# A Strassen scheme with GpSimd weight sums for both MLPs of a hybrid decoder trunk

## The chip, the cores and the metric

One core of a Trainium2 chip runs the whole kernel in one launch. Its engines work side by side, each on its own in-order queue: TensorE (PE), VectorE (DVE), ScalarE (ACT), GpSimd (POOL) and SyncE (SP), which here only issues transfers between DRAM and the on-chip memory. The metric is the device time of one execution in microseconds (us). Three timed runs of the kernel before took 2699.15, 2699.44 and 2701.14 us; the median is 2699.44 us.

## The reference

The input is 1024 tokens of width 1024, in float32. There are two layers, each a mixer and then an MLP, with a norm before and after each part and a sum onto the stream `h`:

```
hn = rms_norm(h, pre_mix_norm[i])
m = ret_ssd_mixer(hn, ...) if i == 0 else s5_mixer(hn, ...)
h = h + rms_norm(m, post_mix_norm[i])
hn = rms_norm(h, pre_mlp_norm[i])
f = jnp.square(jax.nn.relu(hn @ w_up[i])) @ w_down[i]      # w_up 1024 x 4096, w_down 4096 x 1024
h = h + rms_norm(f, post_mlp_norm[i])
```

The mixer of layer 0 has one wide input projection (6672 columns), retention with 4 heads, a state-space part with 16 heads, gates, and an output projection. The mixer of layer 1 (S5) runs a complex diagonal recurrence over the tokens, then `gelu`, then two 1024 x 1024 products, one of which gates the other (the GLU).

## The kernel before, in words

The tokens go through in two blocks of 512. Every large product is made of three fp32r passes over operands that are split into a high and a low part: `split` (L84) copies the tile to fp32r on ACT (L86) and subtracts that from the tile on DVE (L87), and `mm3` (L101) issues the matmuls hi·hi, hi·lo and lo·hi (L103 to L105), each of 128 x 128 by 512 columns. I call these the dense matmuls; there are 10176. Weights come in chunks of half a megabyte: `chunk` (L89) issues one transfer into `raw`, at L93, and splits two tiles of [128, 512], and each tile feeds 12 dense matmuls. `col` makes a product with the weights stationary, `row` one with the activations stationary.

Small work lies beside the large products. `push` registers a generator, and `tick`, which follows each chunk with 5.2 units, advances it a step at a time. The order in which instructions then stand on each engine is the work of the framework's scheduler, which moves an instruction ahead of others whose operands come later. SP holds a single queue in order: an issue that waits for a semaphore holds up every transfer behind it.

The order of stages is: the mixer of layer 0 for block 0 and for block 1 (`mix0`, L544); the MLP of layer 0 for block 0; that of block 1, with the GLU of block 0 put ahead of its last quarter; the MLP of layer 1 for block 0, with the GLU of block 1 inside; the MLP of layer 1 for block 1. `mlp` (L240) works in four quarters of 1024 hidden columns: eight `col` products, relu and square, split into `p2`, then two `row` products that are added into `acc`. A block's hidden values stay on chip. The S5 generator of each block (`s5`, L719) is spread over most of an MLP of 376 us. It goes through eight groups of channels; for each group DVE makes two complex products of six [128, 512] operations (`cmul`, L590 to L597) and eight scans (L762), and then a gelu. The last MLP ends with a column of products tile by tile, so that its norm is taken for one tile of 128 tokens after the other.

GpSimd has only small work: two or three operations on one column for each norm, copies of three columns, and memsets.

## Time and profile before

| | |
|---|---|
| median of three timed runs | 2699.44 us |
| profiled execution: span from the first to the last instruction | 2700.4 us |
| PE busy | 2656.7 us (98%) |
| DVE busy | 1633.3 us (60%) |
| ACT busy | 1128.7 us (42%) |
| POOL busy | 146.1 us (5%) |
| DMA, share of 16 engines | 37.6%, 126 GB/s on average |
[...]

The span is the profiled execution's own time as far as the profile tells it, and it lies within the three timed runs; so nothing has to be added around it. "Busy" counts the time in which at least one instruction of an engine is under way. A busy PE is not PE at its peak, since matmuls overlap. An issue to landing time of a transfer starts when SP issues it and ends when its semaphore rises.

### The profile page before, as it was taken

What the parts mean: (1) busy time and instruction counts of PE and PEld (TensorE: products, weight loads), DVE (VectorE), ACT (ScalarE), POOL (GpSimd) and SP (SyncE); (2) the same over time, 40 slices, a digit from 0 to 9 for tenths busy, and PEclk for the clock granted to TensorE, in tenths of its full rate; (3) what the DMA queues carried; (4) which work ended last, traced back from release to release, by engine and by line L of the source; (5) the groups of instructions that cost most, each with busy time, mean ns of one, the idle gap of its engine ahead of it and who ended that gap; (6) DMA issues with size and microseconds to landing.
All of it is one profiled execution on the core that took longest, in us unless ns stands there. A gap on an engine that the chain in (4) does not pass through costs nothing.

```text
span 2700.4 us, 34267 instructions
## 1 busy us (share of the span) xinstructions
PE 2656.7 (98%) x12424; PEld 2184.6 (81%) x12424; DVE 1633.3 (60%) x3519; ACT 1128.7 (42%) x2047; POOL 146.1 (5%) x374
## 2 busy tenths in 40 slices
PE   7999999999999999999999999999999999999998
PEld 6878878787887778888888888888888888888887
DVE  4657467666647887887464776256377635533334
ACT  4233344333334345543454342365443335444433
POOL 0100111000001010000010000011000001100000
PEclk9999999999999999999999999999999999999999
DMA  5223122522322354444353443255344324432232
GB/s 175 71 86 105 67 86 94 192 82 86 102 77 81 103 192 150 156 167 157 130 204 117 141 156 125 95 179 199 128 152 139 116 93 172 171 126 94 95 101 78
DMA packets 127849, 340.29 MB, mean 126 GB/s; under 512 B 12960, under 2 KB 37792, under 8 KB 127680
## 3 DMA queue, kind: packets, MB, share of 16 engines
q1 hardware_dynamic: 127680, 338.12, 37.6%
q8 instruction: 97, 1.59, 0.2%
q14 instruction: 72, 0.59, 0.1%
HBM read 306.51 MB, written 31.56 MB: 125 GB/s over the span
## 4 chain that ended last, share of the span: by engine, by line
PE 73%; DVE 5%; issue 1%; ACT 1%; DMA 1%; POOL 1%; DVEq 0%; POOLq 0%; ACTq 0%
PE mm L103 22%; PE mm L105 22%; PE mm L104 22%; PE side L748 1%; DVE rope L762 1%; DVE wlo L87 1%; PE side L777 1%; PE side L517 1%; PE side L776 1%; PE side L775 0%; PE side L202 0%; PE side L412 0%; DVE xc L596 0%; POOL sml L134 0%; DVE xc L597 0%
## 5 line engine op out<-in xcount | busy, mean ns | idle before, releaser
L86 ACT CAST whi<-raw 128x512 fp32r<-128x512 f32 x556 | 344.4, 620 | 805.1 <-PE mm L105 454.7
L87 DVE TENSOR_TENSOR wlo<-raw,whi 128x512 fp32r<-128x512 f32 x556 | 381.3, 687 | 420.2 <-ACT whi L86 407.4
L103 PE MATMUL mm<-hT,whi 128*128 128x512 f32 x1472 | 582.6, 396 | 0.7 <-DVE acc L233 0.5
L105 PE MATMUL mm<-hT,wlo 128*128 128x512 f32 x1472 | 580.3, 394 | 0.0
L104 PE MATMUL mm<-hTl,whi 128*128 128x512 f32 x1472 | 577.1, 392 | 0.0
L103 PE MATMUL mm<-whi,p 128*128 128x512 f32 x1248 | 489.2, 392 | 1.7 <-DVE acc L233 1.7
L104 PE MATMUL mm<-wlo,p 128*128 128x512 f32 x1248 | 487.0, 390 | 0.0
L105 PE MATMUL mm<-whi,p 128*128 128x512 f32 x1248 | 486.2, 390 | 0.0
L87 DVE TENSOR_TENSOR wlo<-rs,whi 128x512 fp32r<-128x512 f32 x284 | 195.6, 689 | 281.8 <-ACT whi L86 280.0
L86 ACT CAST whi<-rs 128x512 fp32r<-128x512 f32 x284 | 176.1, 620 | 438.8 <-PE mm L105 306.9
L105 PEld LDWEIGHTS mm<-hT,wlo 128*128 128x128 f32 x1472 | 276.6, 188 | 62.2 <-issue 1.0
L104 PEld LDWEIGHTS mm<-hTl,whi 128*128 128x128 f32 x1472 | 276.7, 188 | 59.5 <-issue 0.5
L103 PEld LDWEIGHTS mm<-hT,whi 128*128 128x128 f32 x1472 | 277.0, 188 | 57.6 <-issue 1.4
L103 PEld LDWEIGHTS mm<-whi,p 128*128 128x128 f32 x1248 | 234.3, 188 | 49.9 <-DVE acc L233 2.2
L105 PEld LDWEIGHTS mm<-whi,p 128*128 128x128 f32 x1248 | 234.3, 188 | 48.9
L104 PEld LDWEIGHTS mm<-wlo,p 128*128 128x128 f32 x1248 | 234.4, 188 | 47.8 <-DVE wlo L87 0.4
L103 PE MATMUL mm<-whi,hT 128*128 128x512 f32 x384 | 155.4, 406 | 0.4 <-ACT whi L86 0.4
L104 PE MATMUL mm<-wlo,hT 128*128 128x512 f32 x384 | 153.3, 399 | 0.5 <-DVE wlo L87 0.5
L105 PE MATMUL mm<-whi,hTl 128*128 128x512 f32 x384 | 152.8, 398 | 0.0
L87 DVE TENSOR_TENSOR p<-tmp,p 128x512 fp32r<-128x512 f32 x128 | 88.1, 688 | 79.7 <-ACT p L86 79.6
L103 PE MATMUL mm<-whi,q 128*128 128x512 f32 x256 | 101.9, 404 | 3.2 <-DVE tmp L434 3.2
L104 PE MATMUL mm<-wlo,q 128*128 128x512 f32 x256 | 101.9, 398 | 1.1 <-DVE wlo L87 1.1
(291 smaller groups left out, 3186.9 us busy)
## 6 DMA issues: line engine op xcount, KB each, us to landing
raw<-in_w_down SPq DMA_DIRECT2D x66, 512.0 KB, 3.3
rs<-in_w_up SPq DMA_DIRECT2D x64, 512.0 KB, 3.3
raw<-in_w_up SPq DMA_DIRECT2D x64, 512.0 KB, 3.2
rs<-in_w_down SPq DMA_DIRECT2D x62, 512.0 KB, 3.3
raw<-in_win_col SPq DMA_DIRECT2D x56, 512.0 KB, 3.3
raw<-in_win_row SPq DMA_DIRECT2D x48, 512.0 KB, 3.2
xt<-h SPq DMA_DIRECT2D x48, 512.0 KB, 4.5
q<-s5m SPq DMA_DIRECT2D x80, 256.0 KB, 2.9
```

The lines of the kernel that those rows point to most:

```text
L86: nc.scalar.copy(hi, src)
L87: nc.vector.tensor_tensor(lo, src, hi.bitcast(F32), op=ALU.subtract)
L103: mm(out, lhs[0], rhs[0], start=first, stop=False)
L104: mm(out, lhs[0], rhs[1], start=False, stop=False)
L105: mm(out, lhs[1], rhs[0], start=False, stop=last)
L517: mm(Y[:, h * 64 : h * 64 + 64], lm[:, h], xd[:, h * 64 : h * 64 + 64], start=True, stop=True)
L748: mm(B[i][:, x], m[i][:, x], u[:, x], start=True, stop=True)
L762: v.tensor_tensor_scan(Z[i][:, x, 1:129], r4, W[i][:, x], Z[i][:, x, 0:1], op0=ALU.mult, op1=ALU.add)
L776: mm(Yv[:, :, x], X[0][:, x], m[3][:, x], start=False, stop=False)
L777: mm(Yv[:, :, x], X[1][:, x], m[4][:, x], start=False, stop=True)
```

## The change

Both MLPs take all 1024 tokens at once. The activations (1024 tokens x 1024) and the weights (1024 x 4096, then 4096 x 1024) are cut into quarters, and the eight products of quarters are replaced by seven over sums of quarters (the Strassen scheme in the form of Winograd). Four of the seven take sums of weights, T1 to T4. They are made by GpSimd (`prep`): 128 steps for each layer, and in each step one transfer of [128, 4, 128] from DRAM, four additions of [128, 128] and one transfer back to DRAM, into `tq`. The tile `prep` has two buffers. The sums of activations are made on DVE: those of the up product by `prenorm_S`, those of the hidden values in `up`, which writes all seven hidden operands to DRAM (`sh`); `up` begins with twenty steps that need block 0 alone (A11·B11 and A12·B21 of ten of its sixteen groups), and finishes the norm of block 1 and its sums (`done`) after them. `down` reads and splits the hidden operands again for each of its seven products; after five of them it hands block 0 to its norm and S5 part, and block 1 after the seventh. The GLUs and the S5 generators no longer lie within an MLP: the S5 part of block 0 lies beside the end of `down` of layer 0, that of block 1 beside the GLU of block 0. Weights now come as tiles of [128, 512] with one transfer each (`wtile`); `raw` has four of them. The buffers of several tags are merged into `k8` and `h2`.

```diff
-            raw=3, whi=3, wlo=3, hT=1, hTl=1, acc=4, xt=2, p2=16, q2=8, nat=8, xc=6, xr=2, tmp=2, lm=2,
-            xx=2, ret=2, kz=2, sml=12, dtt=10, wB=1, rope=2, junk=1, rs=3,
+            raw=4, whi=3, wlo=3, k8=12, xt=2, q2=8, h2=15, lm=2, xx=2, ret=2, kz=2, sml=12, dtt=10, wB=1,
+            rope=2, junk=1, prep=2,
...
+    def wtile(self, src):
+        raw = self.T("raw", [128, 512])
         self.nc.sync.dma_start(raw, src)
+        hi, lo = self.T("whi", [128, 512], F32R), self.T("wlo", [128, 512], F32R)
+        self.split(hi, lo, raw)
+        return hi, lo
...
+    def prenorm_S(self, src, norm, i, b, S):
...
+            self.nc.scalar.copy(a22, P22)
+            v.tensor_tensor(s[0], P21, a22, op=ALU.subtract)
+            v.tensor_tensor(s[2], A11, P21, op=ALU.subtract)
+            v.tensor_tensor(s[1], A11, s[0], op=ALU.subtract)
+            v.tensor_tensor(A12, A12, s[1], op=ALU.subtract)
+            for n, x in (("s3", s[2]), ("s1", s[0]), ("s2", s[1]), ("A22", a22), ("s4", A12)):
...
+    def prep(self, l):
+        nc, g = self.nc, self.nc.gpsimd
+        for u in range(2):
+            for q in range(16):
+                for c in range(4):
+                    s = slice(c * 128, c * 128 + 128)
+                    t = self.T("prep", [128, 4, 128])
+                    nc.sync.dma_start(t, self.a["mlp"][l, u, q, :, :, s].rearrange("b p f -> p b f"))
+                    for d, x in ((0, 1), (1, 3), (3, 0), (2, 3)):
+                        g.tensor_tensor(t[:, d], t[:, d], t[:, x], op=ALU.add)
+                    nc.sync.dma_start(self.tq[l][u, q, :, :, s].rearrange("b p f -> p b f"), t)
+                    yield
...
+    def up(self, l, S, sh, done):
+        ahead = 10
+        def prod(P, g, a, b, first, last):
+            hi, lo = self.wtile(self.weights(l, 0, g, b))
+            for k in range(4):
+                s = slice(k * 128, k * 128 + 128)
+                self.mm3(P, (hi[:, s], lo[:, s]), S[a][k], first and k == 0, last and k == 3)
+            self.tick(2.6)
...
+        for g in range(0, ahead, 2):
+            ahead_of((g, g + 1))
+        done()
+        for g in range(16):
...
+            prod(c, g, "s3", "T3", True, False)
...
+            prod(d, g, "s1", "T1", True, False)
+            v.tensor_tensor(p7, d, p7, op=ALU.subtract)
+            prod(e, g, "s2", "T2", True, True)
+            v.tensor_tensor(V, V, e, op=ALU.subtract)
...
+            for n, x in (("s1", s1), ("s3", A21), ("s2", s2), ("s4", s4)):
+                nc.sync.dma_start(sh[n][g], x)
+
+    def down(self, l, sh, post):
+        def prod(Ps, a, b, first, last):
+            for g in range(0, 16, 2):
+                x = self.K8(F32R)
+                for i in range(2):
+                    raw = self.T("raw", [128, 512])
+                    nc.sync.dma_start(raw, sh[a][g + i])
+                    self.split(x[:, 2 * i], x[:, 2 * i + 1], raw)
+                    w = self.wtile(self.weights(l, 1, g + i, b))
+                    for t in range(4):
+                        s = slice(t * 128, t * 128 + 128)
+                        self.mm3(Ps[t], (x[:, 2 * i, s], x[:, 2 * i + 1, s]), w, first and g + i == 0, last and g + i == 15)
+                    self.tick(2.6)
...
+        self.push(self.prep(0), 128, 600)
...
+        self.up(0, S[0], sh[0], lambda: (self.finish(pre1), self.finish(p[0, 1])))
+        params = self.push(self.s5_params(), 25, 200)
+        self.push(self.prep(1), 128, 560)
...
+        self.down(0, sh[0], post0)
+        for b in range(2):
+            self.finish(s5[b])
+            if b == 0:
+                s5[1] = self.push(s5_run(1), 30, 80)
+            acc = self.glu(y[b])
```

On SP, in the mixer of layer 0 where the input projection's weights come in, the queue of before holds almost nothing but the chunks (names ending in `_row` and `_out` are weights; `lm`, `rope` are small inputs):

```order
L93 DMA raw_492_2250<-in_w_out 128x1024 [waits DMAHW5_49,DMAHW2_49,DVE_49]
L497 DMA lm_738_3288<-cst0_214 128x8x128 [waits DVE_49,PE_49]
L548 DMA rope_942_4247<-in_cos 128x512 [waits DVE_49]
L549 DMA rope_943_4248<-in_sin 128x512 [waits DVE_49]
L93 DMA raw_497_2284<-in_w_out 128x1024 [waits DMAHW3_49,DMAHW1_49,DVE_49]
L93 DMA raw_506_2326<-in_win_row 128x1024 [waits DMAHW4_49,DVE_49]
L93 DMA raw_524_2389<-in_win_row 128x1024 [waits DMAHW5_49,DVE_49]
L93 DMA raw_547_2477<-in_win_row 128x1024 [waits DMAHW1_49,DVE_49]
```

In the changed kernel the same stretch of SP's queue reads like this (`prep` from `in_mlp` is the load of a step's four quarters, `tq0` from `prep` the store of its sums):

```order
L310 DMA prep_518_2476<-in_mlp 128x4x128 [waits DMAHW3_49]
L310 DMA prep_533_2533<-in_mlp 128x4x128 [waits DMAHW5_49]
L101 DMA raw_339_1522<-in_win_row 128x512 [waits DVE_49]
L313 DMA tq0_75<-prep_518_2476 128x4x128 [waits DMAHW6_49,DMAHW1_49,Pool_49]
L101 DMA raw_343_1559<-in_win_row 128x512 [waits DVE_49]
L313 DMA tq0_75<-prep_533_2533 128x4x128 [waits DMAHW7_49,Pool_49]
L310 DMA prep_540_2576<-in_mlp 128x4x128 [waits DMAHW4_49,DMAHW1_49]
L101 DMA raw_346_1565<-in_win_row 128x512 [waits DVE_49]
L310 DMA prep_551_2627<-in_mlp 128x4x128 [waits DMAHW3_49]
L313 DMA tq0_75<-prep_540_2576 128x4x128 [waits DMAHW4_49,Pool_49]
L101 DMA raw_350_1602<-in_win_row 128x512 [waits DMAHW0_49,DVE_49]
L313 DMA tq0_75<-prep_551_2627 128x4x128 [waits DMAHW6_49,Pool_49]
```

Between the weight tiles now stand loads that wait for the landing of an earlier store, and stores that wait for GpSimd (`Pool`). This pattern goes through the whole mixer of layer 0: all 256 steps, those of layer 1 (`tq1`) too, stand ahead of the first weights of `up`, one step to each tile of [128, 512].

On PE, in the S5 part of block 0, the kernel before has 72 or 96 dense matmuls (`mm`) from the transposes of one group of channels (`side` from `nat`, L742) to those of the next. A piece of that:

```order
L105 MATMUL mm_14404<-hT_11908,wlo_14412 128x512
L742 MATMUL side_14453<-c_66,nat_12870 128x128 x4
L103 MATMUL mm_14477<-hT_11908,whi_14480 128x512
L104 MATMUL mm_14477<-hTl_11909,whi_14480 128x512
L105 MATMUL mm_14477<-hT_11908,wlo_14481 128x512
L103 MATMUL mm_14477<-hT_11908,whi_14480 128x512
L104 MATMUL mm_14477<-hTl_11909,whi_14480 128x512
L748 MATMUL side_14460<-xc_14458,q_3007_14443 128x128 x4
L748 MATMUL side_14461<-xc_14458,q_3008_14444 128x128 x4
L105 MATMUL mm_14477<-hT_11908,wlo_14481 128x512
```

In the changed kernel, at the end of `down` of layer 0, the last groups of block 0 follow each other with no dense matmul between them (L920 is the transpose that was L742, L926 was L748, L953 to L955 make the group's output):

```order
L953 MATMUL side_17314<-q_3568_17253,h_3572_17266 128x4x32
L920 MATMUL side_17346<-c_66,k_3298_15994 128x128 x4
L926 MATMUL side_17353<-h_3592_17351,q_3586_17336 128x128 x2
L954 MATMUL side_17314<-q_3569_17254,h_3581_17306 128x4x32
L926 MATMUL side_17353<-h_3592_17351,q_3586_17336 128x128 x2
L926 MATMUL side_17354<-h_3592_17351,q_3587_17337 128x128
L955 MATMUL side_17314<-q_3570_17255,h_3582_17307 128x4x32
```

From the first to the last transposes of a block's S5 part (seven groups) before had 600 dense matmuls for each block; the changed kernel has 264 for block 0 and 202 for block 1. The dense matmuls of the whole program are 9408, where there were 10176.

## Rows read from the trace of the kernel before

**Rows 1.** The page: busy time, share of the span, instructions of each engine.
```profile
PE 2656.7 (98%) x12424; PEld 2184.6 (81%) x12424; DVE 1633.3 (60%) x3519; ACT 1128.7 (42%) x2047; POOL 146.1 (5%) x374
```
**Rows 2.** The page: the chain that ended last, shares of the span by line.
```profile
PE mm L103 22%; PE mm L105 22%; PE mm L104 22%; PE side L748 1%; DVE rope L762 1%; DVE wlo L87 1%; PE side L777 1%; PE side L517 1%; PE side L776 1%; PE side L775 0%; PE side L202 0%; PE side L412 0%; DVE xc L596 0%; POOL sml L134 0%; DVE xc L597 0%
```
**Rows 3.** Six stages: length, busy time (instructions) by engine, PE clock, DMA share, GB/s.
```profile
29.00:505.00 476.00, 469.76 (x2197) 379.34 (x2196) 299.35 (x588) 182.25 (x354) 34.30 (x104) 1.00 0.28 93
505.00:986.00 481.00, 473.34 (x2212) 381.96 (x2211) 331.09 (x748) 188.13 (x368) 39.80 (x107) 1.00 0.32 105
986.00:1362.00 376.00, 375.47 (x1761) 312.74 (x1760) 268.34 (x911) 184.38 (x332) 14.12 (x33) 1.00 0.47 157
1362.00:1852.00 490.00, 487.44 (x2341) 406.17 (x2340) 289.88 (x537) 207.35 (x361) 22.09 (x54) 1.00 0.44 147
1852.00:2341.00 489.00, 487.16 (x2338) 405.42 (x2338) 286.53 (x499) 206.91 (x361) 20.43 (x40) 1.00 0.43 142
2341.00:2691.00 350.00, 350.00 (x1536) 287.99 (x1534) 140.36 (x203) 146.47 (x252) 8.08 (x17) 1.00 0.31 107
```
**Rows 4.** Waits of SP's queue: total us, times, longest.
```profile
SPq L93 <- DVE wlo L87: 1630.7, 353, 13.6
```
**Rows 5.** DMA issues: count, KB each, median us from issue to landing.
```profile
xt<-h SPq DMA_DIRECT2D x48, 512.0 KB, 4.5
...
h<-xt SPq DMA_DIRECT2D x24, 512.0 KB, 3.5
...
s5m<-lm SPq DMA_DIRECT2D x16, 256.0 KB, 2.5
...
xx<-in_s5bc SPq DMA_DIRECT2D x8, 256.0 KB, 2.9
```
**Rows 6.** GpSimd's groups by form: count, busy us, mean ns, idle before.
```profile
L160 POOL TENSOR_TENSOR sml<-sml,c 128x1 f32<-128x1 f32 x32 | 6.1, 191 | 243.7 <-DVE sml L423 243.7
...
L688 POOL MEMSET xc<- 128x512 f32 x8 | 4.2, 528 | 161.6 <-DVE q L594 80.5 <-DVE xc L592 29.4 <-ACT xc L681 24.2
...
L816 POOL MEMSET c<- 128x128 f32 x1 | 0.2, 204 | 0.3 <-POOLq L945 0.3
```
**Rows 7.** The timeline at the start: start us, length us, engine, line.
```profile
9.08 0.19 POOL L158 TENSOR_SCALAR sml<-sml 128x1 f32<-128x1 f32 x1 [8.05 <-ACT junk L169]
...
9.36 0.56 POOL L134 TENSOR_TENSOR sml<-sml,c 128x1 f32<-128x1 f32 x1
...
11.95 1.28 DVE L197 SCALAR_TENSOR_TENSOR acc<-acc,sml,wB 128x1024 f32<-128x1024 f32 x1 [0.72 <-POOL sml L134]
12.00 1.28 POOL L158 TENSOR_SCALAR sml<-sml 128x1 f32<-128x1 f32 x1
```
**Rows 8.** GpSimd's groups between 29 and 986 us, one of them.
```profile
L158 POOL TENSOR_SCALAR sml<-sml 128x1 f32<-128x1 f32 x28 | 9.0, 320 | 237.5 <-ACT junk L169 203.8 <-DVE acc L233 32.3
```
**Rows 9.** DVE's groups by form, those of the S5 part and the split.
```profile
L87 DVE TENSOR_TENSOR wlo<-raw,whi 128x512 fp32r<-128x512 f32 x556 | 381.3, 687 | 420.2 <-ACT whi L86 407.4 <-PE side L742 12.3
...
L762 DVE TENSOR_TENSOR_SCAN rope<-c,rope,xc 128x128 f32<-128x128 f32 x128 | 50.9, 462 | 0.0
...
L594 DVE TENSOR_TENSOR xc<-xc,xc 128x512 f32<-128x512 f32 x32 | 21.8, 681 | 0.0
...
L221 DVE SCALAR_TENSOR_TENSOR nat<-nat,sml,wB 128x512 f32<-128x512 f32 x16 | 11.4, 742 | 3.3 <-POOL sml L163 3.3
...
L784 DVE SCALAR_TENSOR_TENSOR nat<-nat,side 128x512 f32<-128x512 f32 x16 | 11.0, 686 | 7.3 <-ACT nat L783 7.0
...
L781 DVE TENSOR_SCALAR nat<-nat 128x512 f32<-128x512 f32 x16 | 6.8, 427 | 25.0 <-ACT nat L780 25.0
```
**Rows 10.** The timeline at the end.
```profile
2691.30 0.69 DVE L233 TENSOR_TENSOR acc<-mm,acc 128x512 f32<-128x512 f32 x1
...
2694.04 1.42 DVE L221 SCALAR_TENSOR_TENSOR acc<-acc,sml,wB 128x512 f32<-128x512 f32 x2 [2.05 <-POOL sml L134]
2695.37 1.29 DVE L222 TENSOR_TENSOR xt<-xt,acc 128x512 f32<-128x512 f32 x2
```

More of the change, by code (lines that the diff above doesn't have):

```diff
@@ L202, in prenorm_T @@
                     nc.tensor.transpose(P[:, k * 128 : k * 128 + 128], x[:, c : c + 128], self.ident)
-                s = (slice(None), slice(4 * q, 4 * q + 4), slice(t * 128, t * 128 + 128))
-                self.split(hi[s], lo[s], P.rearrange("p (k n) -> p k n", k=4))
+                Ps.append(P.rearrange("p (k n) -> p k n", k=4))
+            yield t, Ps
+    def prenorm_T(self, src, norm, i, hT, early=False):
+        at = []
+        for q in range(2):
+            p, a = self.pair4()
+            hT += p
+            at.append(a)
+        for t, Ps in self.normed(src, norm, i, early):
+            for q in range(2):
+                for hi, lo in at[q](t):
+                    self.split(hi, lo, Ps[q])
+            yield
@@ new lines, in prenorm_S @@
+    def prenorm_S(self, src, norm, i, b, S):
+        v = self.nc.vector
+        if b == 0:
+            at = {}
+            for n in ("A11", "A12"):
+                S[n], at[n] = self.pair4()
+            S["raw"] = []
+            for t, Ps in self.normed(src, norm, i):
+                raw = [self.T("h2", [128, 4, 128]) for _ in range(2)]
+                S["raw"].append(raw)
+                for q, n in enumerate(("A11", "A12")):
+                    self.nc.scalar.copy(raw[q], Ps[q])
+                    for hi, lo in at[n](t):
+                        self.split(hi, lo, raw[q])
+                yield
+            return
+        at = {}
+        for t, (P21, P22) in self.normed(src, norm, i):
+            if not at:
+                for n in ("s3", "s1", "s2", "s4", "A22"):
+                    S[n], at[n] = self.pair4("q2" if n == "A22" else "k8")
+            A11, A12 = S["raw"][t]
+            s = [self.T("h2", [128, 4, 128]) for _ in range(3)]
+            a22 = self.T("h2", [128, 4, 128])
+            self.nc.scalar.copy(a22, P22)
[4 more added lines that the diff above has]
+            for n, x in (("s3", s[2]), ("s1", s[0]), ("s2", s[1]), ("A22", a22), ("s4", A12)):
+                parts = at[n](t)
+                if len(parts) == 1:
+                    self.split(*parts[0], x)
+                else:
+                    for k, (hi, lo) in enumerate(parts):
+                        self.split(hi, lo, x[:, k])
@@ L389, in ret_side @@
         nc, v, mm = self.nc, self.nc.vector, self.nc.tensor.matmul
-        out += [self.T("nat", [128, 512]) for _ in range(4)]
+        o = self.K8()
+        out += [o[:, c] for c in range(4)]
         for hh in range(2):
@@ L462, in conv @@
         nc, v = self.nc, self.nc.vector
-        xr = self.T("xr", [128, 515])
+        xr = self.T("h2", [128, 515])
         if b == 0:
@@ L486, in ssd_side @@
         nc, v, mm = self.nc, self.nc.vector, self.nc.tensor.matmul
-        out += [self.T("nat", [128, 512]) for _ in range(4)]
+        o = self.K8()
+        out += [o[:, c] for c in range(4)]
         S = self.S[g]
@@ L768, in s5 @@
             yield
-            X = [self.T("xc", [128, 4, 128]) for _ in range(2)]
+            X = [self.T("h2", [128, 4, 128]) for _ in range(2)]
             f = lambda y: y[:, :, 0:128]
@@ L880, in run @@
-        del gl["s5"]
-        self.push(after(n1, 1), 2, 60)
-        acc = self.mlp(1, H[4], s5_end(1), free5)
-        post(acc, seq(h3, 0), "post_mlp_norm", 1, str4(out, 0))
-        self.finish(p[5])
-        last = lambda acc: self.postnorm(acc, seq(h3, 1), "post_mlp_norm", 1, str4(out, 1))
-        self.mlp(1, H[5], none, none, last)
+        H = [[], []]
+        self.tq = [self.dr.tile([2, 16, 4, 128, 512], F32, tag=f"tq{l}", name=f"tq{l}") for l in range(2)]
+        self.p1 = self.dr.tile([16, 128, 512], F32, tag="p1", name="p1")
@@ new lines, in run, with pre_S @@
+        names = ("A11", "A12", "A22", "s1", "s2", "s3", "s4")
+        sh = [{n: self.dr.tile([16, 128, 512], F32, tag=f"sh{l}{n}", name=f"sh{l}{n}") for n in names} for l in range(2)]
+        S = [{}, {}]
+        p = {}
+        def pre_S(l, b, src, span):
+            p[l, b] = self.push(self.prenorm_S(src, "pre_mlp_norm", l, b, S[l]), 4, span)
+        self.finish(self.push(self.prenorm_T(seq(x, 0), "pre_mix_norm", 0, H[0], True), 4, 1))
+        self.mix0_setup()
+        self.push(self.prep(0), 128, 600)
@@ L887, in run @@
+        self.up(1, S[1], sh[1], lambda: (self.finish(pre1), self.finish(p[1, 1])))
+        S[1].clear()
+        self.down(1, sh[1], lambda b, acc: post(acc, seq(h3, b), "post_mlp_norm", 1, str4(out, b)))
         self.finish(*list(self.sides))
```

333 lines of the change are left out of this document (190 added, 143 removed).

## The prediction

> **What bounds the kernel now.** I read the busy shares first: PE is busy for 98% of the span, DVE for 60%, ACT for 42%, GpSimd for 5% [rows 1]. The chain of waits says the same: three lines, the dense matmuls L103 to L105, make 66% of it, and no line of another engine has more than 1% [rows 2]. Then the table by stage, because a share of the whole hides stages with different limits. In every stage PE's busy time comes within 7.7 us of the stage's length [rows 3]. The last stage is 1536 dense matmuls and nothing else on PE: 350.0 us, or 0.228 us each, at full clock. So a dense matmul that goes is worth 0.228 us, as long as nothing else sets the pace in its stage. The SP queue tells how much room is left on the side of the weights: its chunks wait for the split that frees a buffer for 1630.7 us in 353 waits [rows 4], so the transfers are early everywhere, and PE is what they wait for in the end.
>
> **The change part by part.** *Removed.* Seven products for eight takes 768 dense matmuls of the MLPs' 6144: 768 x 0.228 = -175 us. That the change does this is certain from the order (9408 for 10176). All rest is what the seven products need beside PE.
>
> *The weight sums, in the mixer of layer 0.* The order puts all 256 steps of `prep` beside the mixer's weights, one to each tile of half a chunk. The mixer's 136 chunks take 957 us, the first two stages in [rows 3], 7.0 us a chunk, in which SP now has to get through two steps as well. A step is a chain: load, four dependent additions, store, and the buffer is loaded again when the store has landed. With two buffers, two steps take one such round. Its parts: a load of 256 KB lands 2.9 us after its issue, a store of the same shape after 2.5 us [rows 5]. The four additions are not in the trace. A two-input operation of one column takes 0.191 us, a memset of 128 columns 0.204 us and one of 512 columns 0.528 us, which is 0.84 ns a column [rows 6]. From below an addition is thus 0.19 + 0.11 = 0.30 us if it streams like a memset; from above, with three streams one behind the other, 0.19 + 0.32 = 0.51 us. I take 0.45, nearer to the upper end since it reads twice. From one dependent GpSimd instruction to the next there are 0.09 us (9.27 to 9.36 us) [rows 7]. GpSimd also waits for DVE: an operation of 0.19 us that starts while DVE runs one with two on-chip inputs takes 1.28 us, exactly as long as that one [rows 7]; in the two mixer stages the mean of this operation is 0.320 us, so 0.13 us of waiting each [rows 8]. Four additions are 4 x 0.54 = 2.2 us without this wait and 2.7 us with it; I take 2.4. With 0.3 us for hand-overs between queues (estimate: three of 0.1 us) the round is 2.9 + 2.4 + 2.5 + 0.3 = 8.1 us. SP is in order: a store that waits for GpSimd holds up the weight tiles behind it, and four `raw` tiles are 14 us of cover, which a steady lag uses up once. So where two steps stand with two tiles, PE gets its tiles every 8.1 us for 7.0. Some 16 chunks have no pair of steps beside them (at the start, at the change of block and at the end, counted in the order), so the 128 pairs of steps share 120 chunks: 128 x 8.1 + 16 x 7.0 = 1149 us for 957, +190 us; GpSimd's queue also holds the norms and the conv's halo copies, which wait for ACT, so I take +200. The bounds: with additions of 0.30 us, no waiting for DVE and hand-overs for nothing the round is 2.9 + 1.6 + 2.5 = 7.0, +50 us (a cost of nothing takes 845 / 128 = 6.6 us); with 0.51 us, the full wait and landings 0.8 us later each it is 10.1 us, +450 us.
>
> [...]
>
> *The S5 parts and the GLU.* DVE needs for one group twelve operations of 0.681 us, eight scans of 0.462 us, and 0.427 + 0.686 + 0.686 us for the gelu [rows 9]: 8.2 + 3.7 + 1.8 = 13.7 us. PE's own part of a group is about 6 us: in the fourth stage PE is busy for 487.4 us, of which 1920 dense matmuls are 437.8, and eight groups share the other 50 [rows 3]. Before, 600 dense matmuls lay between the first and the last transposes of a block, 137 us, and DVE's 96 us for seven groups disappeared beside them. After, there are 264 and 202. Block 0: PE has 60 + 42 = 102 us, DVE 96 us and the splits of 44 tiles at 0.687 us, 30 us: 126 us, 24 us late. Block 1: PE 46 + 42 = 88, DVE 96 + 17 x 0.687 = 108, 20 us late. Nothing covers the ends: block 1 cannot begin before its norm, a store of 3.5 us and a load of 4.5 us [rows 5], about 12 us in all, and after the last group of each block come gelu, transposes and split, about 10 us. Together 24 + 20 + 12 + 20 = 76, +75 us; at least 45 if the ends overlap, 110 if DVE is idle for a tenth of it.
>
> *The start of `up`.* Twenty steps of 12 dense matmuls, 54.7 us, cover the norm of block 1: its tail and way through DRAM, about 15 us, and then four tiles on DVE, each 1.28 us [rows 7], eight operations of 0.69 us and four quarter ones (about 1.1 us), 8 us, 32 us in all, with a quarter of DVE taken by weight splits: 43 us. That is 58 us, and ACT has as much to do: +10 us in each layer, between 0 and +20.
>
> *`up` and `down` themselves.* A group of `up` with five steps is 13.7 us of PE and 15 DVE operations of 0.69 us, 10.3 us; a step of `down` is 2.73 us of PE and two DVE splits, 1.4 us. Both fit, so the work there is hidden by PE. `down` moves 512 KB in 2.73 us, 192 GB/s, and in layer 0 the S5 parameters besides; the third stage ran with 157 GB/s at 0.47 [rows 3]. I take +10 us for late tiles there, up to +40.
>
> *The end.* Before, the last tile of 128 tokens alone was left: from 2691.3 to the end 9 us [rows 10]. Now four tiles finish together: four additions of 0.69 and four times two parts of 0.742 and 0.69 us on DVE [rows 9], 14 us for about 3.5: +10 us.
>
> **The sum**, against the profiled execution's 2700 us, which lies 1 us above the median: 2700 - 175 + 200 + 75 + 20 + 10 + 10 = 2840 us.
>
> **The rivals.** *GpSimd keeps up.* The round is between 6.6 and 7.0 us, or the stores wait so little that four `raw` tiles cover it: the mixer costs 0 to +50 us, the rest stays (75 + 20 + 10 + 10 = 115), and 2700 - 175 + 25 + 115 = 2665 us. For it speaks the room in the queue [rows 4] and that GpSimd is at 5%; against it that even 7.0 us needs both an addition no dearer than a memset and no wait for DVE, of which [rows 7, 8] show some. The point from which it decides is a round of 7.1 us, where the mixer's cost eats up the 60 us that the other terms leave.
>
> *Sharing makes the round much longer.* DVE and GpSimd hold each other up, and the transfers too land later, since `prep` adds 512 KB to a tile's 256 KB. The additions then are 0.75 us each with waiting, 3.0 us, the landings 3.4 and 3.0: 9.7 us, 128 x 9.7 + 112 = 1354, +395 us: 3035 us. For it: the wait in [rows 7]. Against: DVE is busy for only 66% of the two stages, and not always with two on-chip inputs. [...]
>
> **How the numbers follow.** The forecast 0.70, GpSimd keeps up 0.19, much longer 0.11. A measurement tells from no change what is over 0.2%, about 5 us. Forecast's own range: a round of 7.6 to 8.9 us (+125 to +295) with the other terms between 80 and 160 gives 2740 to 2960. Both signs have some chance; the range that should hold 8 in 10 reaches down to the first rival's number and up close to the second's: 2665 to 3010. Faster 0.18 (the first rival but for its worst end, and hardly any of the forecast), same 0.03, slower 0.79.
>
> **What the profile would show.** If I am right: dense matmuls at 0.228 us, 9408 of them; the mixer of layer 0 at about 1150 us with PE busy for some 80% of it, SP's stores into `tq` waiting for GpSimd as its longest waits, GpSimd's additions at about 0.45 us in the mean or more; PE idle by S5's operations of DVE around the GLUs, with some 310 us from the end of `down` to the start of the second `up`. I am wrong if the mixer stays under 1000 us, if additions are 0.3 us, or if weight tiles overtake the stores. Wrong in another way, if PE's granted clock falls below 1.00 where it now pauses: then every stage with pauses would be longer than these terms say.

## The result, and the profile after

The changed kernel takes 3132.57 us (3126.45 to 3137.45, four runs) against 2700.29 us (2699.15 to 2701.58) for the kernel before: 1.159 times as long, 95% interval 1.158 to 1.161. The forecast was 2840 us with a range of 2665 to 3010: the direction is right, the size is not, and the time lies outside the range. The page of the changed kernel, busy time by engine, against [rows 1]:

```profile
PE 2676.1 (85%) x11656; PEld 2131.7 (68%) x11656; DVE 1883.5 (60%) x3919; ACT 1163.8 (37%) x2159; POOL 702.8 (22%) x1410
```

PE is busy for as long as before (2656.7 us) though it has 768 dense matmuls less. The granted clock was 1.00 in every stage before [rows 3]; now it is 0.87 to 0.89 in the stages in which PE is busy for 77 to 82% of the time, 0.97 and 0.98 where it is for 91 and 95%, and 1.00 in the last, where it is for 99.6%. At the lower clock a matmul takes longer: between 44 and 50 us the granted clock is 0.50 and a dense matmul starts 0.43 us after the one before it in the median, between 52 and 66 us it is 1.00 and this takes 0.23 us. The stages of the changed kernel, columns as in [rows 3]: the mixer of layer 0 for both blocks, `up` and `down` of layer 0, S5 and GLU, `up` and `down` of layer 1:

```profile
23.00:711.00 688.00, 531.12 (x2210) 414.82 (x2211) 324.65 (x609) 181.07 (x356) 332.31 (x662) 0.87 0.59 172
711.00:1365.00 654.00, 520.98 (x2213) 410.56 (x2212) 334.36 (x690) 191.37 (x373) 285.28 (x564) 0.89 0.57 167
1365.00:1703.00 338.00, 321.96 (x1379) 257.82 (x1378) 213.32 (x334) 164.48 (x292) 9.83 (x18) 0.98 0.66 217
1703.00:2125.00 422.00, 382.29 (x1771) 305.97 (x1770) 369.32 (x1200) 188.44 (x349) 16.41 (x52) 0.97 0.71 224
2125.00:2460.00 335.00, 273.25 (x1336) 225.22 (x1336) 234.47 (x461) 111.81 (x209) 22.44 (x48) 0.89 0.47 151
2460.00:2799.00 339.00, 323.20 (x1380) 258.20 (x1379) 214.34 (x342) 166.41 (x301) 13.12 (x24) 0.98 0.65 216
2799.00:3115.00 316.00, 314.82 (x1344) 252.34 (x1343) 170.87 (x258) 143.49 (x247) 8.63 (x12) 1.00 0.66 201
```

The mixer of layer 0 takes 1342 us for 957: that is 385 of the 432 us. Its dense matmuls are the same, but PE's granted clock is 0.87 and 0.89 there, a mean over stretches at 1.00 and at 0.50 like those two, and GpSimd is busy for 618 us where it was for 74. The waits of SP's queue in the changed kernel, against [rows 4]:

```profile
SPq L101 <- DVE wlo L93: 457.1, 314, 7.9
SPq L313 <- POOL prep L312: 445.0, 208, 4.0
SPq L310 <- DMA tq<-prep: 170.4, 128, 7.6
SPq L313 <- DMA prep<-in_mlp: 115.3, 100, 6.5
```

Before, weight tiles waited 1630.7 us for a free buffer, so they were early. Now SP also stands at its stores into `tq` (L313) and at the loads of `prep` (L310), and tiles come late: ACT waits 93.4 and 73.8 us for the landing of the input projection's weights (`in_win_row` and `in_win_col`). GpSimd's additions and the landings of `prep` in the changed kernel:

```profile
L312 POOL TENSOR_TENSOR prep<-prep 128x128 f32<-128x128 f32 x1024 | 554.6, 545 | 643.7 <-DMA prep<-in_mlp 584.8
```

```profile
prep<-in_mlp SPq DMA_DIRECT2D x256, 256.0 KB, 3.4
tq<-prep SPq DMA_DIRECT2D x256, 256.0 KB, 2.4
```

The forecast took 2.9 and 2.5 us for the landings and 2.4 us for four additions with their waiting. The loads land half a microsecond later than that; the rest is right, four additions take 2.4 us in the median. What it made of them is not. One passage shows how the pieces lock. GpSimd, then DVE, between 436 and 446 us of the changed kernel, and the next thing that PE waits for (start us, length us, engine, line, and in brackets what the idle time before waited for):

```profile
437.20 2.08 POOL L312 TENSOR_TENSOR prep<-prep 128x128 f32<-128x128 f32 x4 [3.71 <-DMA prep<-in_mlp]
440.21 2.07 POOL L312 TENSOR_TENSOR prep<-prep 128x128 f32<-128x128 f32 x4 [0.92 <-DMA prep<-in_mlp]
442.24 0.19 POOL L165 TENSOR_TENSOR sml<-sml,c 128x1 f32<-128x1 f32 x1
442.51 0.57 POOL L139 TENSOR_TENSOR sml<-sml,c 128x1 f32<-128x1 f32 x1
443.16 0.22 POOL L168 TENSOR_SCALAR sml<-sml 128x1 f32<-128x1 f32 x1
...
436.42 0.18 DVE L598 BATCH_NORM_AGGREGATE sml<-sml 128x2 f32<-128x6 f32 x1
436.82 0.69 DVE L595 SCALAR_TENSOR_TENSOR h<-h,side 128x512 f32<-128x512 f32 x1 [0.21 <-PE side L591]
443.42 0.54 DVE L600 TENSOR_SCALAR k<-side,sml,sml 128x256 f32<-128x256 f32 x1 [5.91 <-POOL sml L168]
443.88 1.28 DVE L93 TENSOR_TENSOR wlo<-raw,whi 128x512 fp32r<-128x512 f32 x2
445.08 0.35 DVE L580 SCALAR_TENSOR_TENSOR ret<-side,c,c 128x128 f32<-128x128 f32 x1
...
445.48 0.70 PE L584 MATMUL side<-k,ret 128*128 128x256 f32 x2 [3.59 <-DVE ret L580]
```

The norm of a retention part (L165, L139, L168) is ready to run at 436.6 us, when DVE's L598 ends. In GpSimd's queue it stands behind eight additions, and the second four wait for their own load: it runs at 442.24. DVE waits 5.91 us for it. Two splits of weight tiles (L93) and a retention operation (L580) stand behind that on DVE, and PE is idle for 3.59 us until L580 is done.

### The profile page after: what moved, and what is told of

It is laid out like the page before. It is cut to its first block, busy times and chain, and to the rows that moved or that the text cites. A ratio compares the mean times of both kernels' runs of the same rounds, so it can differ in the third digit from the quotient of the medians.

```text
span 3134.1 us, 37287 instructions
## 1 busy us (share of the span) xinstructions
PE 2676.1 (85%) x11656; PEld 2131.7 (68%) x11656; DVE 1883.5 (60%) x3919; ACT 1163.8 (37%) x2159; POOL 702.8 (22%) x1410
## 5 line engine op out<-in xcount | busy, mean ns | idle before, releaser
L93 DVE TENSOR_TENSOR wlo<-raw,whi 128x512 fp32r<-128x512 f32 x784 | 553.9, 710 | 555.6 <-ACT whi L92 551.2
L312 POOL TENSOR_TENSOR prep<-prep 128x128 f32<-128x128 f32 x1024 | 554.6, 545 | 643.7 <-DMA prep<-in_mlp 584.8
L108 PE MATMUL mm<-whi,k 128*128 128x512 f32 x1536 | 620.3, 410 | 64.6 <-ACT whi L92 28.5
L109 PE MATMUL mm<-wlo,k 128*128 128x512 f32 x1536 | 626.8, 408 | 34.1 <-DVE wlo L93 33.9
L110 PE MATMUL mm<-whi,k 128*128 128x512 f32 x1536 | 623.7, 407 | 2.7 <-DVE k L93 2.7
L108 PE MATMUL mm<-k,whi 128*128 128x512 f32 x1216 | 493.8, 406 | 55.2 <-ACT whi L92 54.2
L110 PE MATMUL mm<-k,wlo 128*128 128x512 f32 x1216 | 491.1, 405 | 22.1 <-DVE wlo L93 22.0
L109 PE MATMUL mm<-k,whi 128*128 128x512 f32 x1216 | 491.6, 404 | 0.0
L108 PEld LDWEIGHTS mm<-whi,k 128*128 128x128 f32 x1536 | 296.1, 193 | 146.1 <-ACT whi L92 34.0
L109 PEld LDWEIGHTS mm<-wlo,k 128*128 128x128 f32 x1536 | 297.7, 194 | 112.9 <-DVE wlo L93 43.6
L110 PEld LDWEIGHTS mm<-whi,k 128*128 128x128 f32 x1536 | 298.3, 194 | 76.3 <-DVE k L93 5.3
L108 PEld LDWEIGHTS mm<-k,whi 128*128 128x128 f32 x1216 | 234.3, 193 | 117.6 <-ACT whi L92 60.4
L110 PEld LDWEIGHTS mm<-k,wlo 128*128 128x128 f32 x1216 | 233.7, 192 | 83.4 <-DVE wlo L93 28.1
L109 PEld LDWEIGHTS mm<-k,whi 128*128 128x128 f32 x1216 | 233.9, 192 | 54.5 <-issue 0.5
L93 DVE TENSOR_TENSOR k<-raw,k 128x512 fp32r<-128x512 f32 x224 | 153.9, 689 | 102.1 <-ACT k L92 101.0
```

Source lines behind the costliest of these rows:

```text
L93: nc.vector.tensor_tensor(lo, src, hi.bitcast(F32), op=ALU.subtract)
L108: mm(out, lhs[0], rhs[0], start=first, stop=False, skip_group_check=again)
L109: mm(out, lhs[0], rhs[1], start=False, stop=False, skip_group_check=again)
L110: mm(out, lhs[1], rhs[0], start=False, stop=last, skip_group_check=again)
L312: g.tensor_tensor(t[:, d], t[:, d], t[:, x], op=ALU.add)
```

## The experiments

All were run once, next to the kernel before (2699.7 to 2703.6 us). The changed kernel's own four runs differ by 11 us. "The mixer" is always layer 0's, from its first dense matmul to its last. The table gives it in us, to within 1 us, with the whole time; the sections say what was changed.

The scheduler laid out each run's order anew, but for e17 and e18, where an order is imposed. By the traces, e13, e14 and e17 have the changed kernel's order on every engine, and e18 has that of e9. Wherever else the sums or their transfers are kept (e2 to e10, e12, e15, e16), SP's queue at least is in another order than the changed kernel's, so what such a run differs by contains a change of order; what that can be worth is shown by e17 and e18.

| run | whole | mixer | | run | whole | mixer |
|---|---|---|---|---|---|---|
| before | 2700.3 | 957 | | e9 long fills, own order | 2909.1 | 1101 |
| after | 3132.6 | 1342 | | e10 norms off, three buffers | 3076.1 | 1300 |
| e1 no sums | 2772.6 | 979 | | e11 no sums, parameters in up | 2827.0 | 975 |
| e2 transfers issued by GpSimd | 3399.8 | 1594 | | e12 e6, parameters in up | 2975.0 | 1054 |
| e3 transfers alone | 2885.1 | 1085 | | e13 short fills | 2933.4 | 1134 |
| e4 three buffers | 3126.8 | 1328 | | e14 copies | 3004.2 | 1209 |
| e5 additions alone | 3177.7 | 1367 | | e15 e6, more ahead | 2876.3 | 1049 |
| e6 additions on DVE | 2884.2 | 1050 | | e16 e15, S5 under up | 2901.4 | 1050 |
| e7 layer 1's sums later | 3122.3 | 1149 | | e17 long fills, order of after | 3041.2 | 1247 |
| e8 norms off GpSimd | 3116.7 | 1338 | | e18 additions, order of e9 | 3000.9 | 1182 |

### The sums, taken apart

e1, no sums; the products read stored quarters in their place:

```
-        return self.tq[l][u, q, ("T1", "T3", "T4", "T2").index(n)]
+        return self.a["mlp"][l, u, q, ("T1", "T3", "T4", "T2").index(n)]
-        self.push(self.prep(0), 128, 600)
-        self.push(self.prep(1), 128, 560)
```

> The weight sums are left out altogether (prep is not pushed; the four products that want sums read quarters of the weights themselves, with the same sizes), so the output is not the reference's. Theory 1 (the round load, additions, store in SP's in-order queue paces the mixer of layer 0), theory 2 (GpSimd's additions hold up DVE) and theory 3 (the 134 MB of transfers make weight tiles late) all expect the mixer back at about 957 us from 1342, so 3132 - 385 = about 2750 us. What remains above 2700 - 175 = 2525 is then the price of the S5 part, the starts of up, down of layer 0 and the tail. If the loss of the mixer has a cause outside prep (the new buffers, the single tiles of weights), it stays above 1000 us and the total above 2800.

The sums cost 360 us. Without them the kernel is still 72 us slower than before, so the rival "GpSimd keeps up" (2665 us) could not have come out by any speed of the sums.

e3, loads and stores stay, the additions go (`- g.tensor_tensor(t[:, d], t[:, d], t[:, x], op=ALU.add)`):

> The four additions of each step are left out, loads and stores stay in SP's queue; the output is not the reference's. Theory 1: the round is 3.4 + 2.4 + 0.3 = 6.1 us, below the 6.6 us at which it costs nothing; the mixer takes 960 to 1010 us, the total about 2770. Theory 2: the same, about 2750, since no addition is left. Theory 3: the bytes stay, so the mixer stays near 1340 and the total near 3130.

Transfers alone cost 112 us. SP's waits in this run, of its loads for the last store and of its stores for the load, in the first 960 us, show where SP stands (here `prep` is loaded in L310 and stored in L311):

```profile
SPq L311 <- DMA prep<-in_mlp: 286.4, 231, 5.8
SPq L310 <- DMA tq<-prep: 225.4, 225, 5.6
```

Even with nothing to compute SP waits for landings in its own order, with the weight tiles behind.

e5, the additions on two tiles that stay on chip, no transfers (load and store lines taken out):

> Left out: the loads and stores of the weight sums; the same 1024 additions run on GpSimd on two tiles that stay on chip and wait for no transfer, and the products read four of the eight stored quarters in place of the sums. Measure: the two blocks of layer 0's mixer, 957 us before, 1342 us with the change, 979 us without any sums, 1085 us with the transfers alone. Theory A (the round of load, additions and store paces the weight tiles): nothing waits for transfers any more, so 980 to 1000 us. Theory B (the norms and the conv's copies stand in GpSimd's queue behind additions that wait for loads): the additions wait for nothing, a norm is at most 2 to 3 us late, 1000 to 1050 us. Theory C (GpSimd and DVE shut each other out while two on-chip inputs are read): the additions cost what they cost with the change less the transfers' share, 1342 - 106 = 1236 us, and DVE's splits get longer than 0.69 us.

Without a single transfer the additions cost 405 us. That does not settle theory A, though, since most of it is one standstill that the changed kernel does not have. GpSimd and DVE at the start of this run, and then that stretch with the columns of [rows 3]:

```profile
35.79 320.73 POOL L311 TENSOR_TENSOR prep<-prep 128x128 f32<-128x128 f32 x780
...
37.94 318.61 DVE L145 TENSOR_SCALAR dtt<-c 128x16 f32<-128x16 f32 x1
356.46 0.16 DVE L474 TENSOR_SCALAR c<-c 128x16 f32<-128x16 f32 x1
...
36.00:356.00 320.00, 0.86 (x4) 0.30 (x2) 319.52 (x4) 2.34 (x5) 320.00 (x780) 0.50 0.00 1
```

The DVE operation of L145, which takes 0.165 us in the changed kernel, takes 318.61 us here: while GpSimd has these additions one behind the other, it doesn't get in. It ends at 356.55 us, when GpSimd stops at a norm (356.52 us), to wait for DVE. PE works for 0.86 us of these 320. With no transfer to hold them back, 780 of the 1024 additions had gathered there; only some 85 of the 405 us are left for the rest. So the run shows one DVE operation that stayed out over 780 additions in a row, and not how much additions hold DVE up in the changed kernel.

e6, the additions on DVE (`nc.vector` for `g` in L312):

> The additions run on DVE in place of GpSimd; the transfers stay. The order then also puts half of layer 1's sums behind the mixer. A: a round with four additions of about 0.2 us is 3.4 + 0.8 + 2.4 + 0.3 = 6.9 us, no longer than a chunk of PE, so the mixer goes back to that of the transfers alone, about 1085 us or a little more for 100 us more of DVE's time. B: GpSimd's queue is empty again, 1085 to 1110 us. [...] A fourth theory, D (any engine that waits for a load in its own order holds up what stands behind, and on DVE those are the splits themselves): 1200 us or more.

The engine that seemed the fuller one does it for 112 us in all (2884.2 - 2772.6), no more than the transfers alone cost. In its order 98 of the 256 steps lie behind the mixer, so its mixer is not that of e3.

e7, layer 1's sums kept behind the first `up` by a write into their buffers that needs its last tile:

```
+        if l == 0:
+            for _ in range(2):
+                v.tensor_copy(self.T("prep", [128, 4, 128])[:, 0, 0:1], s4[:, 0:1])
```

> The sums of layer 1 are kept behind the first up of layer 0 by a small copy into their buffers; 128 of the 256 steps then lie beside down, S5 and the GLU. A and B: 363 us for 256 steps in the mixer are 182 for 128, so a mixer of about 1160 us; beside down of layer 0 (422 us, where PE waits for DVE and no norm is needed at once) the steps are hidden and cost 0 to 40 us: total 2950 to 3000 us. C: in down DVE is busy for 87%, and 512 additions of 0.55 us that shut it out cost most of that again, +150 to +280 us there: the total stays above 3080 us.

128 steps less in the mixer save 193 us there, and 128 steps beside `down`, S5 and the GLU cost 179 (936 us for 757). The cost goes along with the steps, 1.5 and 1.4 us each, also where no retention norm is near.

### The waits, one by one

e2, the loads and stores issued by GpSimd (`g.dma_start` for `nc.sync.dma_start`):

> The loads and stores of prep are issued from GpSimd's own queue instead of SP's; nothing is left out. Theory 1: no weight tile stands behind a store any more, the mixer falls to 960 to 1020 us and the total to 2750 to 2810. Theory 2 and theory 3 have the same additions and the same bytes: the mixer stays above 1250 and the total above 3030. A variant of theory 1, that it is GpSimd's own queue in which norms and halo copies wait behind additions, also expects little change here, about 3100.

SP is free, and the kernel slower by 267 us: GpSimd needs 0.77 to 0.78 us for each of 512 issues and waits for the landings itself, with the norms behind. This tells nothing of SP alone.

e4, `prep=3` for `prep=2`:

> The tile prep has three buffers instead of two; nothing is left out. Theory 1: three steps share a round of 8.4 to 9.6 us, 2.8 to 3.2 us a step against 3.5 us of PE for a tile: most of the loss goes, mixer 970 to 1100 us, total 2760 to 2890, unless the scheduler uses the room to crowd the steps closer. Theories 2 and 3: no change, 3050 to 3150.

Within 6 us, and the mixer within 14: a third buffer gives next to nothing, which speaks against the round's length as the pace.

e8, the norms and the conv's copies off GpSimd, and the power of -1/2 left out:

```
-        g = self.nc.gpsimd
+        g = self.nc.vector
...
-            nc.gpsimd.tensor_copy(self.halo[:, i], xr[:, 512:515])
+            nc.scalar.copy(self.halo[:, i], xr[:, 512:515])
```

> Left out: the power of -1/2 in the norms, which gives 1 here. The small operations of the norms go to DVE and the conv's halo copies to ACT and DVE, so that in the mixer GpSimd does nothing but the sums. B: nobody waits in GpSimd's queue for the sums any more; what is left is SP's store wait, mixer 1342 to 1100 to 1200 us. A and C: the norms were not what was late, mixer within 30 us of 1342. If the loop of both queues (SP's stores wait for GpSimd, GpSimd's additions wait for SP's loads, DVE waits for norms behind them) is the cause, it is cut here and the mixer falls by more than half of the 257 us that the additions add to the transfers.

Within 16 us, though the passage above shows the norms waiting. e10 does both, in case the two waits replace each other:

> Left out: the power of -1/2 in the norms, which gives 1 here. The small operations of the norms and the conv's copies are off GpSimd, as in the run before, and the sums have three buffers in place of two. Each alone left the mixer of layer 0 within 15 us of 1342. If two waits take each other's place (norms behind the additions, and weight tiles behind stores that wait for the round), both together bring the mixer to 1100 to 1200 us. Theory C (shutting out) says that neither is the cause: 1290 to 1340 us.

56 us of the 247 that the additions make (3132.6 - 2885.1) are to be had by this. The two waits alone don't explain the rest, as far as runs in orders of their own can tell.

### The kind of operation, and the order

e9, a fill of the same length for each addition (the median addition of the changed kernel takes 0.460 us):

```
-                    for d, x in ((0, 1), (1, 3), (3, 0), (2, 3)):
-                        g.tensor_tensor(t[:, d], t[:, d], t[:, x], op=ALU.add)
+                    for d in range(4):
+                        g.memset(t.rearrange("p b f -> p (b f)")[:, 0:432], 0.0)
```

> Left out: the sums themselves. In place of each addition of 128 columns (0.46 us when nothing is in the way) GpSimd fills 432 columns with zeros, which by the rows of 0.204 us for 128 and 0.528 us for 512 columns takes 0.46 us too; loads, stores, their order and every wait stay. Theory C (an addition and DVE's operations shut each other out): a fill reads nothing, so the mixer of layer 0 goes from 1342 us to 1090 to 1160 us, near the 1085 us of the transfers alone. Theory Q (what counts is that GpSimd is taken for about 2 us a step, in which SP's store and the norms behind it wait): the mixer stays at 1300 to 1342 us.

By its numbers theory C. But the scheduler had laid out another order for it. e13 (fills of 128 columns) and e14 (`g.tensor_copy(t[:, d], t[:, x])`) have the changed kernel's order, instruction by instruction:

> Left out: the sums. Each addition is a fill of 128 columns (0.204 us in the trace of before); the order of the instructions on SP and on GpSimd is exactly that of the changed kernel. Theory C (additions take DVE's time): mixer of layer 0 1080 to 1110 us, as with the long fills (1101 us). Rival (the order of weight tiles, loads, stores and norms makes the mixer slow): with the order of the change the mixer stays above 1250 us.

> Left out: the sums. Each addition is a copy of 128 columns on GpSimd, one input read from on chip; same order as the changed kernel. If an operation that reads one input takes DVE's time as an addition does, by as much as it lasts: at 0.3 us each 1024 copies are 300 us of DVE's time, the mixer between 1180 and 1260 us. If only two inputs exclude DVE: 1080 to 1110 us, as with the fills. Rival (order): above 1250 us.

The short fills' mixer, 1134 us, lies between the two theories' ranges, so neither is enough. The copies' 1209 us lie in the range for a copy that takes DVE's time, but a copy is also longer than a short fill, so e14 alone decides nothing. GpSimd's groups of e13, e14 and e17 (below):

```profile
L312 POOL MEMSET prep<- 128x128 f32 x1024 | 210.6, 207 | 767.1 <-DMA prep<-in_mlp 724.6
```

```profile
L312 POOL COPY prep<-prep 128x128 f32<-128x128 f32 x1024 | 372.2, 366 | 691.1 <-DMA prep<-in_mlp 645.7
```

```profile
L317 POOL MEMSET prep<- 128x432 f32 x1024 | 466.0, 459 | 639.3 <-DMA prep<-in_mlp 595.2
```

The scheduler put a fill of 128 columns, a copy and an addition in one and the same order, and fills of 432 columns in another. On the chip the first three take 0.207, 0.366 and 0.545 us in the mean, so the changed kernel's order is also the one for operations of 0.2 us; what lengths the scheduler reckons with is not shown. The last two runs are the missing corners, with the order of all five engines imposed by dependencies that add no wait: e17 has e9's fills in the changed kernel's order, e18 the changed kernel's additions in e9's order.

```
+                for row in order.values():
+                    for x, y in zip(row, row[1:]):
+                        tc.add_manual_dep(traced[y], traced[x].name, nosync, reason="order")
```

> Left out: the sums. Each addition is a fill of 432 columns, 0.46 us, and the order of all instructions on all five engines is that of the changed kernel (imposed by dependencies without waits). Theory C (additions take DVE's time and fills don't): mixer of layer 0 1100 to 1160 us. Rival (time on GpSimd in this order, whatever the operation): by the line through the short fills and the copies (75 us for 0.16 us an operation) 1134 + 0.25 x 470 = 1250 us or more, up to 1342.

> The complete computation with the additions on GpSimd, in the order that the run with long fills had on all five engines (mixer 1101 us there). Theory C: the additions cost what they cost in their own order, mixer 1300 to 1350 us, total about 3100 us. Rival (order): 1100 to 1150 us, total about 2920 us.

| whole time, us | order of the changed kernel | order laid out for the long fills |
|---|---|---|
| fills, 0.46 us | 3041.2 (e17) | 2909.1 (e9) |
| additions | 3132.6 (after) | 3000.9 (e18) |

Both theories are half right, and the halves add up: the order costs 132 us in either row, the addition in place of a fill 91 or 92 us in either column. The fills take 0.460 us in the mean in e9 and 0.459 in e17, the additions 0.570 in e18 and 0.545 in the changed kernel. DVE's splits of the mixer's weights, with additions in the changed kernel and with fills in the same order in e17 (there the line is L94):

```profile
L93 DVE TENSOR_TENSOR wlo<-raw,whi 128x512 fp32r<-128x512 f32 x274 | 204.8, 753 | 361.6 <-ACT whi L92 360.6 <-DMA prep<-in_mlp 0.7
...
L94 DVE TENSOR_TENSOR wlo<-raw,whi 128x512 fp32r<-128x512 f32 x274 | 186.5, 686 | 318.3 <-ACT whi L93 315.9 <-DMA tq<-prep 1.4 <-DMA prep<-in_mlp 0.8
```

So with additions DVE's splits are longer too, 0.753 us for 0.686. e18 is the changed kernel's whole computation, 132 us faster by nothing but the order. Its mixer is 160 us shorter and its first `up` 28 us longer, since 25 of the 256 steps lie beside `up` in this order. Which engine's order, or which of the moved instructions, makes the difference was not separated. GpSimd and DVE in e9, in a passage that answers to the one of the changed kernel above:

```profile
345.18 2.46 POOL L312 MEMSET prep<- 128x432 f32 x5 [2.64 <-DMA prep<-in_mlp]
347.61 0.19 POOL L165 TENSOR_TENSOR sml<-sml,c 128x1 f32<-128x1 f32 x1
347.87 0.57 POOL L139 TENSOR_TENSOR sml<-sml,c 128x1 f32<-128x1 f32 x1
348.39 0.46 POOL L312 MEMSET prep<- 128x432 f32 x1
348.82 0.22 POOL L168 TENSOR_SCALAR sml<-sml 128x1 f32<-128x1 f32 x1
...
349.07 0.54 DVE L600 TENSOR_SCALAR k<-side,sml,sml 128x256 f32<-128x256 f32 x1 [2.50 <-POOL sml L168]
```

In this order the norm stands between the fills of a step, and here DVE waits 2.50 us in place of 5.91.

### The other terms

e11, the S5 parameters pushed when the head of layer 0's `up` is done, in place of beside `down`, without sums:

```
-        self.up(0, S[0], sh[0], lambda: (self.finish(pre1), self.finish(p[0, 1])))
-        params = self.push(self.s5_params(), 25, 200)
+        par = []
+        self.up(0, S[0], sh[0], lambda: (self.finish(pre1), self.finish(p[0, 1]), par.append(self.push(self.s5_params(), 25, 160))))
+        params = par[0]
```

> Left out: the sums, as in the first run (the products read four of the eight stored quarters in their place). The S5 parameters are made beside the second part of layer 0's up in place of its down. Theory: down of layer 0 takes 422 us for 306 us of dense matmuls because DVE has 135 us of parameters there besides the splits and five groups of S5; without them 310 to 340 us, and the 201 us of up grow to 201 to 240 us: 2773 us becomes 2670 to 2710 us. Rival (what is slow in down is the way of its operands through DRAM, 224 GB/s): down stays above 400 us.

`down` falls from 422 to 380 us, and `up` rises by 93. The parameters are part of what is slow in `down`, but only 42 of 116 us, and they are dearer beside `up`. e12 has the same with the additions on DVE:

> The complete computation with the two repairs: additions on DVE (2884 us by themselves) and the S5 parameters beside up. If the parameters are worth 80 us here as in the run before, 2800 us; DVE has the sums of layer 1 beside down as well, so perhaps 2830 us. Slower than the kernel before (2700 us) by either.

91 us slower than e6, for the same reason: the first `up` rises by 107 us and `down` falls by 8. e15 sets `ahead = 16` on e6:

> The complete computation, additions on DVE, and all 16 pairs of products of up's first two kinds go ahead of block 1's norm in place of 10 (87 us of cover for 55). If the starts of up are late because the norm's chain of about 80 us has too little cover: up with its start falls from 346 and 341 us to about 320 each, total 2884 to about 2840 us. If they are late for another reason (the head's own steps are slow): 2870 to 2890 us.

The 32 steps that now stand at the head of the second `up`, 384 dense matmuls or 87.5 us, take 115.9 us: late by 28 us still. The first 384 take 114.5 us in the changed kernel. More cover doesn't help. PE's longest waits in the first 60 us of the second `up` of the changed kernel:

```profile
PE mm L110 <- DVE wlo L93: 11.0, 2, 9.1
```

On DVE the norm's work stands ahead of the weight splits that PE waits for there, and e15 leaves that as it is. e16 puts S5 and the GLU of block 1 beside that head:

```
+        def glu1():
+            self.finish(s5[1])
+            acc = self.glu(y[1])
+            m[1] = post(acc, seq(h2, 1), "post_mix_norm", 1, seq(h3, 1), 0.25)
+            self.finish(m[1])
+            pre_S(1, 1, seq(h3, 1), 16)
+            self.finish(p[1, 1])
+        self.up(1, S[1], sh[1], glu1)
```

> As the run before, and S5 and the GLU of block 1 lie beside the 32 steps at the head of layer 1's up, which need block 0 alone. If what is slow between down and up is S5 without products beside it: 70 to 100 us less than the run before, about 2755 us. If DVE's own time is the limit there (it is busy for 82% of it): 20 to 40 us less. Slower than the kernel before (2700 us) by either.

25 us slower than e15: from the end of layer 0's `down` to the end of the second `up` it takes 713 us for 688, so S5 beside `up` costs more than it saves. None of the 18 runs beats the kernel before; the nearest complete one is e15 at 2876.3 us.

## Why the prediction was wrong

The sum was 2700 - 175 + 200 + 75 + 20 + 10 + 10. By term:

- **-175, dense matmuls removed.** Right: 9408 are left, and the last stage needs 316 us for 1344, 0.235 us each, near to the 0.228 forecast.
- **+200, the weight sums in the mixer.** This is the step that failed, and by itself takes the time out of the range: +385 were measured, of which 22 are there without sums (e1). The place was right; PE is busy for 78% of the stage as forecast (80%), and SP's stores wait for GpSimd. The model was a round of load, four additions and store, 8.1 us, compared with 7.0 us of PE. Its 0.3 us for hand-overs were the author's estimate; at 442.31 us SP issues a store 0.03 us after the second four additions of the passage above. The model failed in three ways. A round shorter than 7.0 us was to cost at most 50 us: transfers without any addition cost 112 (e3). Sharing with DVE was to make four additions longer, 2.4 us for 2.2, and nothing else: the 2.4 us were right, but 1024 additions cost 92 us more than fills of 0.46 us, the median addition's length, and DVE's splits get longer as well (0.753 us for 0.686 in the mixer, after against e17; 0.716 for 0.686 in the whole kernel, e18 against e9). And the order, taken as given and harmless, costs 132 us against the one that the long fills get (e18). The account of the 360 us: transfers 112, GpSimd's time 24 (e9 less e3, each in its own order), kind of operation 92, order 132.
- **The rival "sharing makes the round much longer"** gave the mixer 1354 us, for 1342 measured. That is luck in part: its additions of 0.75 us were 0.545, and the kind of operation is a quarter of the cost (92 of 360 us), not all.
- **+75, S5 and the GLU, with +10 for late tiles in `down`.** `down` of layer 0 and the S5 stages take 758 us in e1 for 482 us of dense matmuls. PE's other work there is some 128 us (estimate: before, MLPs and S5 took 1704 us for 1576 us of dense matmuls, which contains the same work), so some 148 us are lost for 75. The forecast looked at S5 and the GLU alone. Of the S5 parameters it counted the transfers, and left out that DVE now makes them, and most groups of block 0, beside layer 0's `down`: 422 us for 306 us of dense matmuls, with DVE busy for 369 (fourth row of the stages above). e11 shows the parameters as 42 us of it; what makes up the rest was not settled.
- **+20, the starts of `up`.** 27 us each, 54 in all, by another cause than the forecast's: it weighed the norm's chain against cover, but more cover leaves the delay (e15); PE's longest waits there are for weight splits that stand behind the norm on DVE.
- **+10, late tiles in `up` and `down`.** Outside of layer 0's `down` some 19 us more than 0.228 us a dense matmul (201.7 for 197 twice, 316 for 306).
- **+10, the end.** 18.7 us from the start of the last dense matmul for 9.5 before: right.

In all 2700 - 175 + 385 + 148 + 54 + 19 + 9 = 3140 us, for 3136 of the profiled execution. The last sentence of the prediction named the clock as what would make every stage with pauses longer, and the granted clock did fall, to 0.87 to 0.89: PE is busy for 1052 us in the mixer where it was for 943, for the same matmuls. What of the 385 us that makes was not separated from the waits. One sum of the prediction does not come out: its terms at their ends give 2730 to 2980 us where it says 2740 to 2960; the wider range that it states does not rest on this.

## What to carry to other kernels

Idle time of a second vector engine is not free time: here 1024 two-input additions on GpSimd cost 91 or 92 us more than fills of 0.46 us in the same order, and DVE's splits beside them took 0.753 us for 0.686. Price such operations as time taken from the other engine too, and look at what stands behind them in its queue. A scheduler's order is part of a change's cost: here it laid out one order for operations of 0.207 and of 0.545 us, and imposing the one that it made for a longer operation took 132 us off. Two runs differ by one thing alone only if their orders are the same, which the traces tell. Work that has to be hidden needs a stage where the engine that paces it is idle; moving it beside `up`, where PE is busy for 95% of the stage in the changed kernel, was dearer in e11, e12 and e16 (by 54, 91 and 25 us).

## What the runs showed of the hardware that was not expected

- A single-input DVE operation on 16 columns waited 318.61 us behind 780 additions of GpSimd in a row (e5). In that row they start 0.41 us apart without a gap (320.73 us for 780). In the changed kernel the four additions of a step, each of which waits for the one before, start 0.54 us apart with 0.08 us between them, and DVE does get in; that it is the gap that lets it in was not tested.
- Fills of 432 columns on GpSimd take 0.459 and 0.460 us in the mean in two orders, as long as the two memsets of [rows 6] give for that width (estimate: 0.204 us and 304 columns at 0.84 ns). Additions have a median of 0.460 us in the changed kernel and a mean of 0.545, and a mean of 0.570 in e18.
- 1024 additions of 128 columns cost the kernel 112 us on DVE with their transfers, and 360 us on GpSimd, each in the order laid out for it.
